# Weights of a block's mixing part split ahead of time, inside the FFN before it, and kept in DRAM

## The chip, the cores and the metric

The kernel runs on one core of a Trainium2 chip. The metric is the time of one execution on the device in microseconds (us), less is better. The core's engines run side by side, each through its own list of instructions in order: TensorE (PE) multiplies matrices, VectorE (DVE), ScalarE (ACT) and GpSimd (POOL) work elementwise, and SyncE (SP) does nothing but issue DMA transfers. POOL's queue issues a few DMAs as well.

## The reference, cut to what matters

Two transformer blocks run one after the other on 512 latent tokens of 1024 features, in float32, each of two layers. Block 1 is window and full attention with modulation and a SwiGLU FFN; it also carries 256 context tokens through its first layer. Block 2 is, for each layer:

```
hn = rms_norm_2(h, attn_norm[l]);  proj = hn @ w_in[l]
y_a = rwkv7_mixer(proj[..., :RW_IN], ...)                  # 4 heads, a recurrence over tokens
y_b = retention_mixer(proj[..., RW_IN:RW_IN+RET_IN], ...)  # 4 heads, chunks of 128
y_c = mla_mixer(proj[..., RW_IN+RET_IN:], ..., w_q_up[l], w_kv_up[l])   # 8 heads, causal
h = h + concatenate([y_a, y_b, y_c]) @ w_out[l]
hn = rms_norm_2(h, ffn_norm[l]);  gu = hn @ w_gate_up[l]
h = h + (silu(gu[..., :D_FF_2]) * gu[..., D_FF_2:]) @ w_down[l]
```

The first half of this, up to the product with `w_out`, is called the mixing stage below; `D_FF_2` is 2816, which is 22 tiles of 128.

## The kernel before

Every projection is done as three products of rounded operands: a weight w is split into a high part (rounded to the matmul's format) and a low part (the rest), the activations likewise, and TensorE sums hi·xh, hi·xl and lo·xh. A weight tile is 128 x kt x 128; with kt = 8, which most have, it is 512 KB and takes 24 matmuls of 128x512. `load_w` (line 129) fetches one: SP's DMA brings it into one of RAW_BUFS = 2 staging buffers `raw`, ACT casts it into `whi` (line 140), DVE subtracts `raw - whi` into `wlo` (line 141). There are W_BUFS = 3 slots for `whi` and `wlo` each, and an instruction that writes into a slot waits until the slot's last readers are done; the raw buffer is free again when line 141 has read it.

The **FFN** (`ffn`, line 919) takes the 22 tiles of its inner dimension in two parts, PARTS2 = 14 and 8. For each inner tile it loads a gate and an up tile (two `load_w`), multiplies both (48 matmuls of 128x512 in the FFNs spoken of here), and `swiglu` turns the two results into a split activation on ACT, DVE and, in block 2, POOL. Behind each part, `residual` multiplies the part's activations by the down weights, 8 output tiles.

The **mixing stage** of block 2 fetches its weights through a list: `orders(l)` names 33 tiles in the order of their use, `order_w` sets the list, and `next_w` (line 148) returns the next tile and keeps three fetched:

```
while self.coming and len(self.loaded) < 3:
    self.loaded.append(self.load_w(self.coming.pop(0)))
return self.loaded.pop(0)
```

Seven more (`w2in` tiles 6, 2, 3, 0, 1, 4, 5, the inputs of the RWKV part) go through `w2proj` straight to `load_w`. Of the 40 tiles of a layer 30 are 512 KB, four (`w2kn`) 128 KB, six (`w2qr`, `w2qn`) 192 KB. The last eight, `w2out`, are the product with `w_out`; three of these are held half multiplied in the banks `b` before the last inputs are there, and finished together (line 1950).

Within an engine the order of the instructions is the order in which the program issues them; waits between engines and for DMAs come from the tiles' readers and writers. The layers' FFNs are spread over the time as follows: the FFN of block 1's layer 1 takes 1508 to 1926 us, block 2's first mixing stage from there to about 2230, its FFN 2258 to 2630, the second mixing stage to about 2930, and the last FFN the rest.

Of the kernel before, what the change touches and what calls it, by code (L numbers as in the profile page):

```python
# [10 lines left out]
F32 = mybir.dt.float32  # L11
F32R = mybir.dt.float32r
# [10 lines left out]
KD = 8  # L23
# [4 lines left out]
TM_BUFS, QS_BUFS, RAW_BUFS, W_BUFS = 5, 3, 2, 3  # L28
# [11 lines left out]
class Seg:  # L40


    def __init__(self, key, off, n):
        self.key, self.off, self.n = key, off, n
        self.v = 0 if key == "lat" else 1
# [12 lines left out]
class Kern:  # L58
    def __init__(self, tc, d, out, ctx, V):
        self.tc, self.nc, self.d, self.out = tc, tc.nc, d, out  # L60
        self.ctx, self.V = ctx, V
        nc = self.nc
        self.uid = 0
        E = ctx.enter_context
        self.const = E(tc.tile_pool(name="const", bufs=1))
        self.wp = E(tc.tile_pool(name="wp", bufs=2))
        self.tmp = E(tc.tile_pool(name="tmp", bufs=2))
        self.dram = E(tc.tile_pool(name="dram", bufs=1, space=DRAM))
        c = self.const
        self.vec = c.tile([128, d["vec"].shape[1]], F32, name="vec")  # L70
        nc.sync.dma_start(out=self.vec, in_=d["vec"])
        self.cf = c.tile([128, d["cf"].shape[1]], F32, name="cf")
        nc.sync.dma_start(out=self.cf, in_=d["cf"])
        self.ident = self.cf[:, 0:128]
        self.ones = self.cf[:, 128:129]
        self.bones = self.cf[:, 129:131]
        self.nhalf = self.cf[:, 131:139]
        self.identb = c.tile([128, 128], BF16, name="identb")
        nc.vector.tensor_copy(self.identb, self.ident)
        self.mge = c.tile([128, 128], BF16, name="mge")  # L80
        self.mle = c.tile([128, 128], BF16, name="mle")
        for o, m in ((0, self.mge), (128, self.mle)):
            t = self.tm(128)
            nc.sync.dma_start(out=t, in_=d["cm"][:, o:o + 128])
            nc.vector.tensor_copy(m, t)
        self.ahead = []
        self.banks = {}
        self.lo = "vector"
        self.lb = itertools.cycle("lb")
        self.pend = []  # L90
        self.stream = "L"


    def pool(self, es, name, side=None):
# [46 lines left out]
        getattr(self.nc, self.lo).tensor_tensor(lo, raw, hi.bitcast(F32), op=ALU.subtract)  # L141
        return hi, lo

    def order_w(self, aps):

        self.coming, self.loaded = list(aps), []

    def next_w(self):

        while self.coming and len(self.loaded) < 3:  # L150
            self.loaded.append(self.load_w(self.coming.pop(0)))
        return self.loaded.pop(0)

    def split(self, x, hi, lo):
# [755 lines left out]
    def ffn(self, wgu, wd, H, x, gcol, segs, start, last, parts, done, ada=0, scales=None, norm=None, after=None, pre=None, angles=False):  # L910


        bc = None
        f0 = 0
        keys = [s.key for s in segs]
        for pi, nf in enumerate(parts):
            with ExitStack() as es:
                pool = self.pool(es, "act")
                act = self.feat(pool, nf, keys, F32R, "ah"), self.feat(pool, nf, keys, F32R, "al")
                wait = []  # L920
                todo = [(f, segs) for f in range(nf)]
                if pi == 0:
                    todo = start + todo[1 + max((f for f, _ in start), default=-1):]
                for i, (f, sg) in enumerate(todo):
                    wg, wu = (self.ahead.pop(0) if self.ahead else self.load_w(wgu[f0 + f, i]) for i in range(2))
                    for s in sg:
                        pg, pu = self.bank()[:, :s.n], self.bank()[:, :s.n]
                        self.proj([(wg[0], wg[1], range(KD))], H, s, pg)
                        if norm:
                            next(norm)  # L930
                        self.proj([(wu[0], wu[1], range(KD))], H, s, pu)
                        if norm:
                            next(norm)
                            norm = None
                        wait.append((s, f, pg, pu))
                        if scales:
                            bc = next(scales)
                            if bc is None:
                                continue
                            scales = None  # L940
                        for s, f_, pg, pu in wait:
                            self.swiglu(s, pg, pu, bc, s.of(act[0], f_), s.of(act[1], f_))
                        wait = []
                    if f0 + f > 1:
                        self.ada_some(ada)
                    if angles and f0 + f == 2:
                        self.angles()
                end = pi == len(parts) - 1
                if callable(gcol):
                    gcol = gcol()  # L950
                self.residual(lambda n, k0, kn: wd[n][:, f0 + k0:f0 + k0 + kn], nf, act, x, gcol,
                              last if end else self.plan(segs), done if end else None, after() if end and after else None, pre if end else None)
                f0 += nf
# [16 lines left out]
    def block1(self):  # L970
        nc, d = self.nc, self.d
        es_ada = ExitStack()
        self.adap = self.pool(es_ada, "ada", "right")
        for l in range(2):
            segs = [LAT, CTX] if l == 0 else [LAT]
            keys = [s.key for s in segs]
# [105 lines left out]
            if l == 0:  # L1082
                def after():
                    nonlocal A, sh
                    A, sh = self.mod_cols(1, 0)
                    return self.mod_norm(X, accs, LAT, A, sh, H, "b", "b")

                self.ffn(d["wgu0"], d["wd0"], H, X, gt, segs, start, self.plan(segs, segs, 5), [7, 7, 8], done, ada=3, norm=norm, after=after,
                         pre=lambda: self.ahead.append(self.load_w(d["wqk1"][0])))
            else:  # L1090
                gf, ga = (self.vec[:, self.V[nm]:self.V[nm] + KD] for nm in ("final", "attn_norm"))
                g = self.one(self.const, [128, KD], F32, "gfa")
                nc.vector.tensor_tensor(g, gf, ga, op=ALU.mult)
                self.acc = self.one(self.tabp, [128, T], F32, "acc2")
                self.acc2 = [accs["lat"], self.acc]
                done = lambda s, n: self.prepare(s, n, X, g, H, [(accs["lat"], None), (self.acc, gf)], True)
                self.xd = self.dram.tile([KD, 128, T], F32, name="xd")
                self.ffn(d["wgu1"], d["wd1"], H, X, gt, segs, start, self.plan([LAT]), PARTS2, done, norm=norm, angles=True)
            es_ps.close()
        self.X = X  # L1100
# [141 lines left out]
        return self.run(self.w2proj_steps(l, j, H, tag, False))  # L1242

    def w2proj_steps(self, l, j, H, tag=None, ordered=True):
        w = self.next_w() if ordered else self.load_w(self.d[f"w2in{l}"][j])
        ps = self.bank(tag or next(self.lb))
        yield from self.proj_steps([(w[0], w[1], range(KD))], H, LAT, ps)
        return ps
# [451 lines left out]

    def orders(self, l):

        d = self.d
        w = d[f"w2in{l}"]
        return ([w[16], w[17], w[18], w[13]] + [d[f"w2kn{l}"][p] for p in range(4)] + [w[14], d[f"w2kvv{l}"], w[15], w[7]]
                + [d[f"w2qr{l}"][p] for p in range(2)] + [d[f"w2qn{l}"][p] for p in range(4)] + [w[9], w[8], w[10]]
                + [d[f"w2v{l}"][c] for c in range(2)] + [w[11], w[12]] + [d[f"w2out{l}"][n] for n in range(KD)])

    def retention(self, l, pool, src, mix):

# [130 lines left out]
    def block2(self):  # L1841
        nc, d = self.nc, self.d
# [27 lines left out]
        for l in range(2):  # L1870
# [89 lines left out]
            def token_scales():  # L1960
                r = self.inv_sqrt(self.token_sums([self.acc], "b")[:, 0:4], 1.0 / 1024)
                yield None
                self.spread(r, "b", bcf)
                yield bcf

            nxt = gcols("attn_norm", 1) if l == 0 else None
            if l == 0:
                done = lambda s, n: self.prepare(s, n, X, nxt, H, [acc], True)
                self.ffn(d[f"w2gu{l}"], d[f"w2d{l}"], H, X, None, [LAT], [], self.plan([LAT]), PARTS2, done, scales=token_scales())
            else:  # L1970
# [217 lines left out]
```

## Time and profile before

| | |
|---|---|
| median of 3 runs | 3361.28 us (3359.95 to 3367.67) |
| profiled execution | 3356.82 us |
| its span, first to last instruction | 3355.1 us |
| PE busy | 3281.2 us (98%) |
| DVE busy | 1901.4 us (57%) |
| ACT busy | 1231.0 us (37%) |
| POOL busy | 355.9 us (11%) |
| DMA, mean | 115 GB/s |

Busy is the time in which an engine worked on an instruction; the share is of the span. The profiled execution lies 1.5 us above its span and 4.5 us under the median of the runs. The DMA share of a stretch, used further down, is the mean busy share of the core's 16 DMA engines in it.

### The profile page before, as it was taken

The numbers are of one execution on the slowest core, as the hardware profiler recorded it, in microseconds if no ns is written. First come the engines' busy times: TensorE is split into PE (matmuls) and PEld (weight loads), VectorE is DVE, ScalarE is ACT, GpSimd is POOL, SyncE is SP. The second block draws the span as 40 slices with busy tenths as digits, with TensorE's granted clock in tenths as the row PEclk, the third lists the DMA queues.
The fourth block names the chain that finished last, engine by engine and source line by source line (L and its number), as shares of the span: only waits on it lengthen the run. The fifth ranks groups of instructions, "written<-read, shape, count | busy, mean of one in ns | idle before, by whom it ended". The sixth has DMA issues, their size and how long they took to land. (4 is left out here: it accounts for less than half of the span.)

```text
span 3355.1 us, 48931 instructions
## 1 busy us (share of the span) xinstructions
PE 3281.2 (98%) x19460; PEld 2741.7 (82%) x19460; DVE 1901.4 (57%) x3324; ACT 1231.0 (37%) x2192; POOL 355.9 (11%) x340
## 2 busy tenths in 40 slices
PE   7999999999999999999999999999999999999998
PEld 4888888888888888889888877778888777788887
DVE  4767765756444567757333466764434566754343
ACT  3566632311212346734222432542223332632222
POOL 0131100100000101101000211121001101121001
PEclk9999999999999999999999999999999999999999
DMA  5533372334434243253232323433333323422322
GB/s 205 147 125 119 114 266 106 114 119 132 126 126 132 76 135 110 93 181 115 94 91 98 123 71 105 130 100 93 91 94 100 109 68 98 133 94 94 91 98 82
DMA packets 137533, 385.86 MB, mean 115 GB/s; under 512 B 17428, under 2 KB 29204, under 8 KB 137304
## 3 DMA queue, kind: packets, MB, share of 16 engines
q1 hardware_dynamic: 133976, 372.15, 35.0%
q0 software_dynamic: 3328, 10.57, 1.0%
q8 instruction: 153, 2.51, 0.3%
q14 instruction: 76, 0.62, 0.1%
HBM read 331.56 MB, written 43.76 MB: 112 GB/s over the span
## 5 line engine op out<-in xcount | busy, mean ns | idle before, releaser
L140 ACT CAST whi<-raw 128x1024 fp32r<-128x1024 f32 (+4 forms) x432 | 435.0, 1008 | 1265.0 <-PE b L159 825.4
L141 DVE TENSOR_TENSOR wlo<-raw,whi 128x1024 fp32r<-128x1024 f32 (+4 forms) x427 | 508.6, 1192 | 379.6 <-ACT whi L140 372.5
L159 PE MATMUL b<-hh,whi 128*128 128x512 f32 (+1 forms) x1760 | 686.8, 390 | 0.0
L159 PE MATMUL b<-hh,wlo 128*128 128x512 f32 (+1 forms) x1760 | 686.0, 390 | 0.0
L159 PE MATMUL b<-hl,whi 128*128 128x512 f32 (+1 forms) x1760 | 681.7, 387 | 0.2 <-POOL hl L251 0.2
L159 PEld LDWEIGHTS b<-hh,whi 128*128 128x128 f32 x1760 | 332.3, 189 | 74.1 <-issue 4.6
L159 PEld LDWEIGHTS b<-hl,whi 128*128 128x128 f32 x1760 | 332.2, 189 | 73.3 <-issue 0.6
L159 PEld LDWEIGHTS b<-hh,wlo 128*128 128x128 f32 x1760 | 332.1, 189 | 72.3 <-issue 0.3
L159 PE MATMUL b<-ah,whi 128*128 128x512 f32 (+1 forms) x864 | 316.7, 367 | 0.0
L159 PE MATMUL b<-al,whi 128*128 128x512 f32 (+1 forms) x864 | 316.5, 366 | 0.0
L159 PE MATMUL b<-ah,wlo 128*128 128x512 f32 (+1 forms) x864 | 316.3, 366 | 0.0
L967 DVE TENSOR_TENSOR tm<-tm,b 128x512 f32<-128x512 f32 (+1 forms) x112 | 70.0, 625 | 206.1 <-PE b L159 200.1
L159 PEld LDWEIGHTS b<-ah,whi 128*128 128x128 f32 x864 | 163.0, 189 | 28.1
L159 PEld LDWEIGHTS b<-ah,wlo 128*128 128x128 f32 x864 | 163.0, 189 | 28.0
L159 PEld LDWEIGHTS b<-al,whi 128*128 128x128 f32 x864 | 163.0, 189 | 27.9
L428 DVE SCALAR_TENSOR_TENSOR wlo<-raw,silb 128x1024 f32<-128x1024 f32 x128 | 158.7, 1240 | 36.6 <-DMA raw<-in_ada1b 20.1
L159 PE MATMUL l<-hh,whi 128*128 128x512 f32 (+1 forms) x472 | 176.7, 374 | 0.9 <-DVE stB L717 0.3
L159 PE MATMUL l<-hh,wlo 128*128 128x512 f32 (+1 forms) x472 | 173.1, 367 | 0.5 <-DVE wlo L141 0.5
L159 PE MATMUL l<-hl,whi 128*128 128x512 f32 (+1 forms) x472 | 173.1, 367 | 0.0
L528 DVE TENSOR_TENSOR pt<-t,pt 128x384 fp32r<-128x384 f32 (+2 forms) x272 | 131.1, 511 | 35.8 <-ACT pt L527 34.1
L159 PE MATMUL b<-hc,whi 128*128 128x256 f32 x800 | 145.4, 283 | 0.0
L159 PE MATMUL S<-kst,qst 128*128 128x256 f32 (+2 forms) x576 | 138.2, 344 | 2.9 <-DVE S L568 1.2
(558 smaller groups left out, 5673.1 us busy)
## 6 DMA issues: line engine op xcount, KB each, us to landing
raw<-in_wgu SPq DMA_DIRECT2D x92, 512.0 KB, 3.3
raw<-in_w2gu SPq DMA_DIRECT2D x88, 512.0 KB, 3.4
raw<-in_ada1b SPq DMA_DIRECT2D x48, 512.0 KB, 3.3
raw<-in_w2in SPq DMA_DIRECT2D x38, 512.0 KB, 3.7
raw<-in_ada0b SPq DMA_DIRECT2D x32, 512.0 KB, 3.8
raw<-in_wg SPq DMA_DIRECT2D x32, 512.0 KB, 3.8
raw<-in_w2d SPq DMA_DIRECT2D x32, 512.0 KB, 3.5
raw<-in_wd SPq DMA_DIRECT2D x24, 512.0 KB, 3.6
```

The source lines that it names most:

```text
L140: self.nc.scalar.copy(hi, raw)
L141: getattr(self.nc, self.lo).tensor_tensor(lo, raw, hi.bitcast(F32), op=ALU.subtract)
L159: self.nc.tensor.matmul(out, l, r, start=start, stop=stop)
L428: nc.vector.scalar_tensor_tensor(junk, raw, 0.5, self.silb[:, v], op0=ALU.mult, op1=ALU.mult, accum_out=m[:, w, k, v:v + 1])
L528: nc.vector.tensor_tensor(o, src, h.bitcast(F32), op=ALU.subtract)
L967: nc.vector.tensor_tensor(b, th, pu, op=ALU.mult)
```

## The change

In two FFNs, that of block 1's layer 1 and that of block 2's layer 0, each inner tile from the third on (20 of 22) is followed by `halve_some(2)`: two tiles of the next mixing stage are loaded and split by `load_w` as before, into the same raw buffers and slots, and POOL's queue writes the high and the low part to DRAM (`kh`, `kl`). So all 40 tiles of a layer are split in the FFN before it. In the mixing stage `load_k` takes the place of `load_w`: two DMAs of SP bring the high and the low part from DRAM straight into a slot of `whi` and one of `wlo`, with no raw buffer, no cast and no subtraction. The other FFNs, which have nothing to split, and block 1 are as before.

```
+        self.halves, self.to_halve = {}, []
...
+    def halve_some(self, n):
+
+        for _ in range(min(n, len(self.to_halve))):
+            key = self.to_halve.pop(0)
+            w = self.load_w(self.weight(key))
+            kept = self.halves[key] = [self.dram.tile([128, w[0].shape[1], 128], F32, name=f"{nm}_{'_'.join(map(str, key))}") for nm in ("kh", "kl")]
+            for a, b in zip(kept, w):
+                self.nc.gpsimd.dma_start(out=a, in_=b.bitcast(F32))
...
+    def load_k(self, key):
+
+        kept = self.halves[key]
+        kt = kept[0].shape[1]
+        w = [self.t(self.wp, [128, 8, 128], F32R, nm, W_BUFS)[:, :kt] for nm in ("whi", "wlo")]
+        for a, b in zip(w, kept):
+            self.nc.sync.dma_start(out=a.bitcast(F32), in_=b)
+        return w
...
-            self.loaded.append(self.load_w(self.coming.pop(0)))
+            self.loaded.append(self.load_k(self.coming.pop(0)))
...
                     if f0 + f > 1:
                         self.ada_some(ada)
+                        self.halve_some(2)
...
+                self.to_halve = [("w2in", 0, j) for j in (6, 2, 3, 0, 1, 4, 5)] + self.orders(0)
                 self.ffn(d["wgu1"], d["wd1"], H, X, gt, segs, start, self.plan([LAT]), PARTS2, done, norm=norm, angles=True)
...
-        w = self.next_w() if ordered else self.load_w(self.d[f"w2in{l}"][j])
+        w = self.next_w() if ordered else self.load_k(("w2in", l, j))
...
+                self.to_halve = [("w2in", 1, j) for j in (6, 2, 3, 0, 1, 4, 5)] + self.orders(1)
                 done = lambda s, n: self.prepare(s, n, X, nxt, H, [acc], True)
                 self.ffn(d[f"w2gu{l}"], d[f"w2d{l}"], H, X, None, [LAT], [], self.plan([LAT]), PARTS2, done, scales=token_scales())
```

Three places in the lists of instructions show the order that comes out of it. The name of a buffer carries a running number; what an instruction waits for stands behind it (DMAHW a DMA of SP, DMASW one of POOL's queue). The first place is ACT's list in the FFN of block 1's layer 1, from the middle of an inner tile on. Before:

```order
L140 CAST whi_15928<-raw_15926 128x1024 [waits DMAHW7_49,PE_49,Activation_49]
L155 CAST ah_15405<-tm_15792 128x512 [waits DVE_49]
L140 CAST whi_15934<-raw_15932 128x1024 [waits DMAHW0_49,PE_49,Activation_49]
L963 ACTIVATE tm_15919<-b_15869 128x512 [waits PE_49]
L140 CAST whi_15997<-raw_15995 128x1024 [waits DMAHW1_49,PE_49,Activation_49]
```

and now:

```order
L141 CAST whi_15948<-raw_15946 128x1024 [waits DMAHW1_49,PE_49]
L141 CAST whi_15958<-raw_15956 128x1024 [waits DMAHW2_49,PE_49,Activation_49]
L988 ACTIVATE tm_15939<-b_15889 128x512 [waits PE_49]
L141 CAST whi_15968<-raw_15966 128x1024 [waits DMAHW3_49,DMASW4_49,DVE_49]
L141 CAST whi_15974<-raw_15972 128x1024 [waits DMAHW4_49,DMASW6_49,DVE_49]
L179 CAST ah_15406<-tm_15940 128x512 [waits DVE_49]
L141 CAST whi_16037<-raw_16035 128x1024 [waits DMAHW5_49,PE_49]
L988 ACTIVATE tm_16028<-b_15978 128x512 [waits PE_49]
L141 CAST whi_16047<-raw_16045 128x1024 [waits DMAHW6_49,Activation_49]
L141 CAST whi_16057<-raw_16055 128x1024 [waits DMAHW7_49,DMASW0_49,DVE_49]
```

Two casts an inner tile have become four: 15948 and 15958 are tiles of the mixing stage, 15968 and 15974 the gate and up tiles of the next inner tile. These two go into the slots that 15948 and 15958 had, and so wait for their writes to DRAM (DMASW4, DMASW6). The writes stand in POOL's list, at the same inner tile:

```order
L152 DMA kh_w2in_3_15952<-whi_15948 128x1024 [waits Activation_49]
L152 DMA kl_w2in_3_15953<-wlo_15949 128x1024 [waits DVE_49]
L152 DMA kh_w2in_0_15962<-whi_15958 128x1024 [waits Activation_49]
L152 DMA kl_w2in_0_15963<-wlo_15959 128x1024 [waits DMASW7_49,DVE_49]
L152 DMA kh_w2in_1_16041<-whi_16037 128x1024 [waits DMASW0_49,Activation_49]
```

They are new, and are issued in the order in which the casts and subtractions are done. The third place is SP's list at the end of block 2's first mixing stage, where the first three `w2out` tiles are in the slots and the fourth comes. Before, its raw load (`raw_21308`) stands 34 rows ahead of these rows, which fetch the fifth to the seventh:

```order
L1926 DMA tm_21261<-mix_17981 128x512 [waits DMAHW0_49,DVE_49]
L134 DMA raw_21389<-in_w2out 128x1024 [waits DMAHW1_49,DVE_49]
L134 DMA raw_21426<-in_w2out 128x1024 [waits DMAHW2_49,DVE_49]
L134 DMA raw_21463<-in_w2out 128x1024 [waits DMAHW1_49,DVE_49]
```

and now the fourth itself stands here, in two DMAs:

```order
L1951 DMA tm_21593<-mix_18381 128x512 [waits DMAHW3_49,DVE_49]
L165 DMA whi_21638<-kh_w2out_3_17856 128x1024 [waits DMAHW4_49,PE_49]
L165 DMA wlo_21639<-kl_w2out_3_17857 128x1024 [waits DMAHW5_49,PE_49]
L165 DMA whi_21664<-kh_w2out_4_17935 128x1024 [waits PE_49]
L165 DMA wlo_21665<-kl_w2out_4_17936 128x1024 [waits DMAHW7_49,PE_49]
L165 DMA whi_21715<-kh_w2out_5_17945 128x1024 [waits DMAHW0_49,PE_49]
```

What waited for a raw buffer (DVE) now waits for a slot, that is for the matmuls of the tile that was in it (PE).

## Rows read from the trace of the kernel before

**Rows 1.** The page: busy time, share of the span, instructions of each engine

```profile
PE 3281.2 (98%) x19460; PEld 2741.7 (82%) x19460; DVE 1901.4 (57%) x3324; ACT 1231.0 (37%) x2192; POOL 355.9 (11%) x340
```

**Rows 2.** Stretches: length, busy time of each engine, clock, DMA share, GB/s

```profile
core 0: us, PE busy (x) PEld busy (x) DVE busy (x) ACT busy (x) POOL busy (x), PEclk, DMA share, GB/s
1580.00:1711.00 131.00, 131.00 (x574) 105.95 (x574) 51.25 (x60) 36.90 (x48) 0.00 (x0) 1.00 0.30 99
...
1940.00:2112.00 172.00, 164.97 (x1695) 126.02 (x1694) 115.84 (x283) 53.37 (x89) 16.98 (x22) 1.00 0.30 90
2112.00:2230.00 118.00, 109.50 (x761) 90.11 (x762) 86.52 (x184) 65.14 (x158) 16.96 (x13) 1.00 0.38 111
2640.00:2930.00 290.00, 274.17 (x2412) 215.14 (x2411) 192.91 (x459) 116.68 (x245) 37.69 (x37) 0.96 0.33 98
14.00:24.00 10.00, 9.06 (x36) 5.42 (x36) 1.64 (x4) 0.72 (x2) 1.02 (x1) 1.00 1.03 411
440.00:492.00 52.00, 49.07 (x281) 42.52 (x280) 39.83 (x68) 16.47 (x31) 0.00 (x0) 1.00 0.90 304
800.00:1000.00 200.00, 200.00 (x1157) 177.24 (x1156) 101.29 (x156) 42.26 (x60) 0.00 (x0) 1.00 0.41 132
```

**Rows 3.** Timeline of ACT, block 1's second FFN: start, duration, instruction [idle before]

```profile
1594.87 0.61 ACT L155 CAST ah<-tm 128x512 fp32r<-128x512 f32 x1
1599.51 1.05 ACT L140 CAST whi<-raw 128x1024 fp32r<-128x1024 f32 x1 [4.03 <-issue]
...
1606.07 0.61 ACT L155 CAST ah<-tm 128x512 fp32r<-128x512 f32 x1
```

**Rows 4.** Timeline of DVE there

```profile
1600.59 1.22 DVE L141 TENSOR_TENSOR wlo<-raw,whi 128x1024 fp32r<-128x1024 f32 x1 [3.77 <-ACT whi L140]
```

**Rows 5.** DMA issues, whole execution: count, KB each, median us to landing

```profile
raw<-in_wgu SPq DMA_DIRECT2D x92, 512.0 KB, 3.3
...
raw<-in_w2out SPq DMA_DIRECT2D x16, 512.0 KB, 4.4
...
y0a<-yt POOLq DMA_DIRECT2D x4, 384.0 KB, 2.6
...
y0b<-yt POOLq DMA_DIRECT2D x4, 384.0 KB, 3.6
```

**Rows 6.** DMA in 430 to 492 us, a busy stretch: total, issues

```profile
DMA packets 7304, 19.00 MB, mean 306 GB/s; under 512 B 768, under 2 KB 1792, under 8 KB 7301
...
raw<-in_ada0b SPq DMA_DIRECT2D x7, 512.0 KB, 4.1
gl<-gates SPq DMA_DIRECT2D x4, 768.0 KB, 6.5
raw<-in_wp SPq DMA_DIRECT2D x6, 512.0 KB, 4.5
```

**Rows 7.** DMA issues in 800 to 1000 us, block 1's first FFN

```profile
raw<-in_ada1b SPq DMA_DIRECT2D x25, 512.0 KB, 3.3
```

**Rows 8.** DVE, first mixing stage, by line: count, busy, mean ns, idle

```profile
L141 DVE TENSOR_TENSOR wlo<-raw,whi 128x1024 fp32r<-128x1024 f32 x21 | 26.4, 1257 | 17.5 <-ACT whi L140 17.5
```

**Rows 9.** Waits of PE in the first mixing stage: total us, times, longest

```profile
PE l L159 <- DVE wlo L141: 0.4, 1, 0.4
```

**Rows 10.** Chain that ended last, in the second mixing stage: start, us, what

```profile
2812.68 1.06 ACT whi L140
2813.76 1.23 DVE wlo L141
...
2842.02 1.23 DVE wlo L141
...
2859.24 0.94 ACT whi L140
```

**Rows 11.** Timeline of PE where the fourth w2out tile begins

```profile
2229.48 0.40 PE L159 MATMUL b<-ml,whi 128*128 128x512 f32 x1
...
2230.63 0.50 PE L159 MATMUL b<-mh,wlo 128*128 128x512 f32 x1
```

More of the change, by code (lines that the diff above doesn't have):

```diff
@@ L142, in load_w, with weight, order_w @@
         return hi, lo
-    def order_w(self, aps):
-        self.coming, self.loaded = list(aps), []
+    def halve_some(self, n):
[5 more added lines that the diff above has]
+                self.nc.gpsimd.dma_start(out=a, in_=b.bitcast(F32))
+    def weight(self, key):
+        name, l, i = key
+        w = self.d[f"{name}{l}"]
+        return w if i is None else w[i]
+    def load_k(self, key):
[5 more added lines that the diff above has]
+        return w
+    def order_w(self, keys):
+        self.coming, self.loaded = list(keys), []
     def next_w(self):
         while self.coming and len(self.loaded) < 3:
-            self.loaded.append(self.load_w(self.coming.pop(0)))
+            self.loaded.append(self.load_k(self.coming.pop(0)))
         return self.loaded.pop(0)
@@ L1701, in orders @@
     def orders(self, l):
[L1703 to L1707, printed above, removed]
+        w = lambda *j: [("w2in", l, i) for i in j]
+        some = lambda nm, n: [(nm, l, i) for i in range(n)]
+        return (w(16, 17, 18, 13) + some("w2kn", 4) + w(14) + [("w2kvv", l, None)] + w(15, 7) + some("w2qr", 2) + some("w2qn", 4)
+                + w(9, 8, 10) + some("w2v", 2) + w(11, 12) + some("w2out", KD))
     def retention(self, l, pool, src, mix):
```

## The prediction

> **What bounds the kernel now.** I read the page first: PE is busy in 98% of the span, DVE in 57%, ACT in 37% [rows 1]. So time can be gained only where PE waits, and lost wherever something new makes it wait. Then the stretches, because the average hides where the 2% lie. In the FFN of block 1's layer 1, 131 us hold 131.00 us of PE: nothing to gain there, and ACT (36.90) and DVE (51.25) have room. The first mixing stage holds 164.97 of 172 and 109.50 of 118 us, so PE is idle for 7.0 + 8.5 = 15.5 us; the second 274.17 of 290, so 15.8 [rows 2]. What the change can gain is at most these two idle times. What it can lose is in the two FFNs, where PE has no gap and 80 tiles' worth of work is put in.
>
> **What it removes: the splits in the mixing stages.** Per stage 40 casts and 40 subtractions go. The 21 large subtractions in the first stage are 26.4 us of DVE [rows 8], a fifth of its busy time there [rows 2]. But work of DVE is not time of PE: of PE's waits in that stage only one is put down to a split, for 0.4 us [rows 9]. The splits act in another way, by standing in the queues of DVE and ACT ahead of small steps of the RWKV recurrence, on which PE waits. The chain of waits shows that: it covers the second half of the second mixing stage (from 2784 us on), and has four pieces of splits in it, 1.06 + 1.23 + 1.23 + 0.94 = 4.5 us [rows 10]. Twice that for the whole stage is 9; when a piece leaves the chain, the next late thing (another step of the recurrence on DVE, or a transfer through DRAM) takes some of its place, and I take two thirds: 6 us a stage. The bounds are 0 (the one wait of 0.4) and 15.5 (all of the idle time).
>
> **What it changes in the mixing stages: the loads.** A tile now comes in two transfers instead of one, 17.4 MB more in about 290 us (30 x 0.524 + 4 x 0.131 + 6 x 0.197), some 60 GB/s on top of 98 where 411 have been moved [rows 2]: hidden, while three tiles are fetched ahead. The cost is that a tile can't be fetched at all until a slot is free; before, the raw buffer took it early. That bites where three slots are let go at once, at the fourth `w2out` tile, whose two DMAs now wait for the last matmuls of the first three. Each of these ends with three matmuls, one tile behind the other, so the first slot is free six matmuls, 6 x 0.233 = 1.4 us, before PE wants the fourth. The high part lands 3.3 us after that, with little beside it [rows 5], the low part behind it: 2 x 0.524 MB at 411 GB/s are 2.55 us, and 3.3 less the 1.28 that 0.524 MB take is 2.0, so 4.6. PE uses the low part only in its third matmul, 0.47 us on: 4.6 - 1.4 - 0.5 = 2.7 us of idle. Before, the same place has 1.15 us from the one start to the other for three matmuls that take 0.70 [rows 11], a loss of 0.45. So about +2.3 a stage; bounds 0, if PE has another wait there anyway, and 4.4 (both parts landing in the 4.4 of `w2out` now [rows 5], one after the other). A stage then gives -6 + 2.3 = -3.7, both **-7.4 us**.
>
> **What it adds in the FFNs.** Per inner tile two more tiles go through the two raw buffers, so each buffer carries two loads a tile. A buffer is in use from the issue of its load until the subtraction has read it, and only then is the next load issued. With R the time to landing, the cast 1.05 us [rows 3], the subtraction 1.23 [rows 4, 10] and 0.04 between them, one use is R + 2.32, and an inner tile can't take less than 2 x (R + 2.32). PE needs 11.2 us for its 48 matmuls (the same ACT instruction at 1594.87 and at 1606.07 [rows 3]). So R decides:
> - R = 3.3, as gate and up tiles land now [rows 5]: 11.24 us, as good as hidden. The lower bound, +0.
> - R = 4.1 to 4.5, as 512 KB land in the stretch that moves 306 GB/s [rows 6]: with 4.3, 13.24 us, +2.0 a tile.
>
> Which R applies follows from the load: an inner tile moves eight times 0.524 MB (gate, up, two raw tiles, four writes), 4.19 MB. In 11.2 us that is 374 GB/s, four times the 99 of now [rows 2], and more than any stretch but the first few microseconds has (411 in 14 to 24 us). In 13.24 us it is 317 GB/s, near the 306 in which R was 4.3. The two agree with each other, so I take **+2.0**. For the upper bound: 4.19 MB at 306 GB/s are 13.7 us, and one cast of 1.05 that no longer lies beside a transfer makes it 14.7, +3.5.
>
> The writes themselves are behind this: the slot of a written tile is wanted by the subtraction of the next gate or up tile, R + 1.05 = 5.3 us after the written tile's own subtraction. POOL's queue lands 384 KB in 2.6 and 3.6 us [rows 5]; for 512 KB I take 4.1, the upper of them and half a microsecond, which is 1.2 inside. ACT stays below its limit: four casts and two other instructions an inner tile (4 x 1.05 + 1.2 = 5.4 of 13 us); DVE likewise. But ACT is in order: a cast that waits for its load holds up the activation of the gate result behind it, and through it the release of PE's banks, so the lateness of a load reaches PE by that way also.
>
> The 20 inner tiles with splits are 13 with two large tiles, 4 with a large and a small one, 3 with two small ones: by the order of the list (seven `w2in`, four more, four `w2kn`, and so on). With 2.0, 1.0 and 0 for these an FFN loses 13 x 2.0 + 4 x 1.0 = 30 us, both **+60**; bounds 0, and 2 x (13 x 3.5 + 4 x 1.75) = 105. The `residual` parts have no splits.
>
> **The sum.** 60 - 7.4 = 52.6 us. On the profiled execution, 3356.8, that is 3409.4; it lies 4.5 us under the median of the runs, so on the median 3361.3 + 52.6 = **3414 us**. All bounds to one side give 3361.3 - 31.3 = 3330 and 3361.3 + 105 + 8.8 = 3475.
>
> **The rivals.**
> - *The loads stay hidden, and little changes.* In block 1's first FFN up to three more loads of 512 KB an inner tile run beside the gate and up tiles, and land in 3.3 us all the same [rows 7], with PE at 200 of 200 us [rows 2]. Against it: that stretch moves 132 GB/s, a third of what the split FFNs would. With R of 3.3 to 3.5 an FFN loses 0 to 6 us, and the time is 3361.3 - 7.4 + 0 to 12, 3354 to 3366: no measurable change. [...]
> - *Faster.* The same R, and the mixing stages give more than I take, since a fifth of DVE's work is gone from the stages in which the recurrence runs through DVE. The point from which it decides: 10 us a stage of the 15.5 idle ones, with 2.3 lost at `w2out`; two stages give -15, 3346 us. For it speaks that RWKV steps stand right behind a split in the chain; against it the one wait of 0.4 us [rows 9], and above all that the FFNs must lose nothing.
> - *Much slower: the writes come one at a time.* If POOL's queue starts a write only when the one before has landed, an inner tile needs 4 x 4.1 = 16.4 us, +5.2, and 2 x 4.1 + 2 x 2.5 = 13.2 with one small tile, +2.0. Two FFNs lose 2 x (13 x 5.2 + 4 x 2.0) = 151, and the time is 3361.3 + 151 - 7.4 = 3505 us. For it: the two kinds of POOL writes differ by 1.0 us for the same size [rows 5]. Against it: nothing in the list makes a write wait for its neighbour, only for the one eight before. The Trainium skill (SBUF — State Buffer, section "SBUF: two separate sides") warns that GpSimd can't write the descriptors of its DMAs while DVE runs in a mode that takes both ports, so that such a DMA stands still behind DVE; a subtraction of two tensors is not among the operations that the page names for it, and no run here shows such a stall.
>
> **How the numbers follow.** A change of under 0.3%, 10 us, can't be told from none here (3351 to 3371). My forecast, slower by 10 to about 105 us: 0.68. Much slower, over 105: 0.11. Within 0.3%: 0.11. Faster: 0.10. So faster 0.10, same 0.11, slower 0.79. The range from 3352 to 3470 leaves out most of the faster case and most of the much slower one, together just under 2 in 10; the forecast's own range, from R of 3.7 (2 x 6.02 = 12.04, +0.84 a tile, +25 in all, 3379) to the bandwidth's 13.7 (+2.5 a tile, +75, 3429), is 3379 to 3429.
>
> **What would show it.** In the two FFNs, in the stretches 1580 to 1711 and 2253 to 2375 moved by what is lost before them: an inner tile of 13.2 us instead of 11.2, PE idle before a gate's or up's first matmul, that idle time put down to `wlo` or `whi`, and these to the load of `raw`; gate tiles landing in about 4.3 us; some 317 GB/s; the writes landing within 5.3 us. In inner tiles 8, 12 and 13 no loss. In the mixing stages: no row of line 140 or 141, each about 4 us shorter, and 2 to 3 us of PE idle at the fourth `w2out` tile that waits for a DMA of `kl`. What would make me wrong: landing at 3.3 us in the FFNs (then there is no loss), writes that land late (then the wait at the cast is for POOL's queue, and the tile longer than 14), or a mixing stage that shortens by over 10 us.

## The result and the profile after

The changed kernel takes 3490.1 us (median of 4 runs, 3482.04 to 3490.61) against 3360.6 of the kernel before beside it: a ratio of 1.038, 95% interval 1.0367 to 1.0393, so 129.5 us slower. The forecast was 3414 us (3352 to 3470): the sign was right, the size well outside the range.

The page of the changed kernel, to be held against [rows 1]: the span, the engines, and the software queue, which is POOL's and now carries the writes.

```profile
span 3488.5 us, 49608 instructions
...
PE 3334.2 (96%) x19460; PEld 2767.5 (79%) x19460; DVE 1904.0 (55%) x3324; ACT 1236.8 (35%) x2192; POOL 440.6 (13%) x500
...
q0 software_dynamic: 22912, 80.31, 6.2%
```

PE does the same 19460 matmuls, and is busy 53 us longer: many ran at the lower level of the clock. The rest of the loss is idle time of PE. To see where the time went I compared the start of the same matmul in both traces; in the FFNs PE's list of matmuls is the same. Up to 1570 us of the kernel before the two keep within 2 us. Then the changed kernel falls (times of the kernel before) 61.0 us behind in the first FFN with splits (up to 1930), 7.7 more in the mixing stage (up to 2250), 60.7 in the second FFN (up to 2630), 4.9 in the second mixing stage, and nothing after it. So 121.7 of the 132 us between the traces are in the two FFNs, and the mixing stages give nothing back. I call how much later a matmul starts than in the trace of before its lateness.

Stretches of the changed kernel, columns as in [rows 2]: the two parts of the first FFN, the two of the second.

```profile
1605.00:1745.00 140.00, 121.07 (x468) 93.09 (x469) 60.98 (x70) 46.83 (x60) 21.83 (x41) 0.91 0.70 234
1825.00:1952.00 127.00, 107.25 (x428) 81.94 (x427) 56.18 (x60) 44.43 (x53) 17.02 (x32) 0.95 0.77 263
2310.00:2490.00 180.00, 163.65 (x655) 127.81 (x654) 88.38 (x99) 61.17 (x76) 47.87 (x57) 0.93 0.64 215
2615.00:2721.00 106.00, 88.70 (x330) 66.99 (x329) 55.10 (x57) 38.00 (x44) 23.96 (x33) 0.90 0.79 266
```

Where PE had 131.00 of 131 us, it now has 121 of 140 and 107 of 127, at a granted clock of 0.90 to 0.95 of the full 2.4 GHz. Part of each stretch ran at the lower level, 1.2 GHz, always in or just behind a wait of PE.

What the waits and what the clock cost can be read apart. The same matmuls of the two FFNs, from the third inner tile to the last down product, before:

```profile
1582.70:1926.50 343.80, 343.80 (x1491) 279.33 (x1490) 133.64 (x149) 98.85 (x127) 20.54 (x13) 1.00 0.32 103
2282.00:2629.80 347.80, 347.80 (x1491) 279.76 (x1490) 155.35 (x174) 98.58 (x123) 38.76 (x29) 1.00 0.32 99
```

and in the changed kernel:

```profile
1580.90:1985.70 404.80, 364.18 (x1491) 286.20 (x1490) 171.10 (x188) 133.37 (x164) 62.98 (x97) 0.95 0.66 219
2348.90:2757.50 408.60, 373.90 (x1492) 291.20 (x1491) 195.17 (x212) 131.64 (x161) 85.05 (x109) 0.95 0.66 215
```

Of the 121.8 us between them PE stands idle for 40.6 + 34.7 = 75.3, and for 20.4 + 26.1 = 46.5 it is busy longer with the same matmuls. A granted clock of 0.95 over 813 us is worth about 41 of these 46.5.

### The profile page after: what moved, and what is told of

It reads as the page before. It is cut to its first block, busy times and chain, and to the rows that moved or that the text cites. A ratio compares the mean times of both kernels' runs of the same rounds, so it can differ in the third digit from the quotient of the medians.

```text
span 3488.5 us, 49608 instructions
## 1 busy us (share of the span) xinstructions
PE 3334.2 (96%) x19460; PEld 2767.5 (79%) x19460; DVE 1904.0 (55%) x3324; ACT 1236.8 (35%) x2192; POOL 440.6 (13%) x500
## 5 line engine op out<-in xcount | busy, mean ns | idle before, releaser
L183 PE MATMUL b<-hh,whi 128*128 128x512 f32 (+1 forms) x1760 | 700.6, 398 | 49.4 <-ACT whi L141 49.4
L183 PE MATMUL b<-hh,wlo 128*128 128x512 f32 (+1 forms) x1760 | 698.1, 397 | 18.5 <-DVE wlo L142 18.4
L183 PE MATMUL b<-hl,whi 128*128 128x512 f32 (+1 forms) x1760 | 692.1, 393 | 0.2 <-POOL hl L275 0.2
L511 DVE TENSOR_REDUCE st<-S 128x1 f32<-128x768 f32 (+2 forms) x160 | 121.9, 764 | 33.7 <-PE S L183 32.8
```

What stands on the lines that cost most here:

```text
L183: self.nc.tensor.matmul(out, l, r, start=start, stop=stop)
L511: nc.vector.tensor_reduce(nm, S[:, lo:hi], axis=AX.X, op=ALU.max, negate=True)
```

## Inside one inner tile of the changed kernel

The forecast's loop can be read from three engines' lists, at an inner tile of the first FFN's second part. ACT (start, duration, instruction, idle before and what ended it):

```profile
1863.62 1.04 ACT L141 CAST whi<-raw 128x1024 fp32r<-128x1024 f32 x1 [3.49 <-DMA raw<-in_wgu]
...
1869.62 1.05 ACT L141 CAST whi<-raw 128x1024 fp32r<-128x1024 f32 x1 [1.12 <-DMA raw<-in_w2in]
...
1876.52 1.05 ACT L141 CAST whi<-raw 128x1024 fp32r<-128x1024 f32 x1 [2.41 <-DMA raw<-in_wgu]
```

DVE:

```profile
1864.70 1.23 DVE L142 TENSOR_TENSOR wlo<-raw,whi 128x1024 fp32r<-128x1024 f32 x1 [3.21 <-ACT whi L141]
...
1870.70 1.23 DVE L142 TENSOR_TENSOR wlo<-raw,whi 128x1024 fp32r<-128x1024 f32 x1 [0.87 <-ACT whi L141]
...
1877.82 1.23 DVE L142 TENSOR_TENSOR wlo<-raw,whi 128x1024 fp32r<-128x1024 f32 x1 [2.45 <-DMA kl_w2in<-wlo]
```

SP's issues (the time runs from the first issue of a row to the end of the second):

```profile
1865.95 3.63 SPq L135 DMA_DIRECT2D raw<-in_w2in  x2
1871.95 3.78 SPq L135 DMA_DIRECT2D raw<-in_wgu  x2
1879.07 5.16 SPq L135 DMA_DIRECT2D raw<-in_w2out  x2
```

One raw buffer goes through these rows: DVE has read it at 1864.70 + 1.23 = 1865.93, the next load is issued at 1865.95, cast at 1869.62 and read at 1871.93; the load behind that is issued at 1871.95 and cast at 1876.52. Its subtraction then doesn't start with the cast's end (1877.57) but at 1877.82, when the write of a low part (`kl_w2in`) has landed. Two uses, 1865.95 to 1879.07, take 13.1 us. That is the loop of the forecast at its forecast length, 13.2, and this tile (PE 1864.7 to 1878.0) made PE 2.1 us late, near the 2.0 expected. But it is the shortest of those that lose anything. The eight tiles of this part added 0, 0, 6.3, 2.1, 6.6, 2.6, 3.6 and 5.7 us of lateness. DMA in that part, 1856 to 1950 us (mean busy share in 40 slices, then the median us to landing):

```profile
DMA  9999738999945379985499997389989259998817
...
raw<-in_wgu SPq DMA_DIRECT2D x10, 512.0 KB, 5.2
raw<-in_w2out SPq DMA_DIRECT2D x8, 512.0 KB, 3.8
kh_w2out<-whi POOLq DMA_DIRECT2D x8, 512.0 KB, 5.4
kl_w2out<-wlo POOLq DMA_DIRECT2D x8, 512.0 KB, 6.6
```

The waits from 1850 to 1950 us (total us, times, longest):

```profile
ACT whi L141 <- DMA raw<-in_wgu: 26.6, 9, 6.1
...
PE b L183 <- ACT whi L141: 15.7, 6, 5.6
DVE wlo L142 <- DMA kl_w2out<-wlo: 11.5, 3, 6.2
...
ACT whi L141 <- DMA kh_w2out<-whi: 6.1, 1, 6.1
```

A low part's write lands 6.6 us after its issue, a high part's 5.4, and four of them (two casts and two subtractions lie next to each other) meet the two gate and up loads, which land in 5.2. The three long tiles end in two ways. At the end of the tile that adds 6.6 us a gate's cast waits 6.1 us for a high part's write and the subtraction behind it 6.2 for a low part's; PE waits 5.64 us. The other two end with a late load: the gate's load that closes the tile of 6.3 us is issued at 1856.73, when its raw buffer comes free, and lands 6.8 us later; the first down load behind the tile of 5.7 us takes 7.0. PE behind the first of these waits:

```profile
1895.74 0.80 PE L183 MATMUL b<-hh,whi 128*128 128x512 f32 x1 [5.64 <-ACT whi L141]
...
1898.26 0.63 PE L183 MATMUL b<-hl,whi 128*128 128x512 f32 x1
1898.69 0.63 PE L183 MATMUL b<-hh,wlo 128*128 128x512 f32 x1
...
1899.43 0.39 PE L183 MATMUL b<-hl,whi 128*128 128x512 f32 x1
1899.66 0.39 PE L183 MATMUL b<-hh,wlo 128*128 128x512 f32 x1
```

Behind the wait matmuls start 0.43 us apart, at the lower level of the clock, then 0.23 apart again. The DMA engines, meanwhile, go from 90% and more down to 10 or 20% and back: transfers in a heap, then the splits, with hardly a transfer beside them.

## The theories

1. **Staging** (the forecast's): the two raw buffers, each used twice an inner tile, make the loop.
2. **Slots**: the next gate and up tiles wait until the writes out of their slots have landed.
3. **Bytes**: eight transfers of 512 KB an inner tile are more than the DMA engines move in 11.2 us.
4. For the mixing stages: the splits taken out were worth 6 us a stage (forecast), or had been hidden already.

This table gives the lateness that PE gains within the inner tiles of the two FFNs, in us, worked out as above from each run's trace (without what it gains between the parts, 7.5 us in the changed kernel). The last column stops at the part's last matmul and the second at the first one behind it; up to there the last has 2.9 more in the changed kernel, 1.0 in x_w2, 3.5 in d_act and 1.5 in w_hi:

```
                                         FFN 1         FFN 2
                                     part 1 part 2  part 1 part 2    sum
changed kernel                         32.6   26.9    30.7   24.0   114.2
x_w2     own slots                     26.1   22.5    24.9   21.1    94.6
d_act    writes on ACT's queue         24.7   18.3    30.9   22.9    96.8
x_r2     own raw buffers               12.7   16.8    19.9   16.6    66.0
w_q      a quarter of each write        9.8   15.3    18.5   14.9    58.5
w_hi     high part written only        11.3   10.1    18.1    9.3    48.8
x_r2w2   own raw buffers, 2 slots       2.3   14.9     1.6   15.6    34.4
x_r2w3   own raw buffers, 3 slots       0.5   14.9     0.0   13.1    28.5
f_nowr   no writes                      0.0    0.0     6.0    2.3     8.3
one      one tile per inner tile        0.0    0.0     7.6    0.0     7.6
x_r2w2q  own buffers, quarter writes    1.1    4.0     0.0    0.0     5.1
```

## The experiments

m_only, m_noout, one and x_r2w2 were timed four times or more, the other variants once. The kernel before varied from 3354.8 to 3367.7 us over 21 runs, so a single time is good to some 10 us; the argument goes by the table, which compares traces. In m_only, m_noout, w_q and x_r2w2q the mixing stages read one kept tile in place of all, and in w_hi its low part, as the expectations say, so they measure time alone.

**m_only: the mixing part alone.**

```
-                self.to_halve = [("w2in", 0, j) for j in (6, 2, 3, 0, 1, 4, 5)] + self.orders(0)
+                self.to_halve = [("w2in", 0, j) for j in (6,)]
...
-        kept = self.halves[key]
-        kt = kept[0].shape[1]
+        kt = self.weight(key).shape[1]
+        kept = [k[:, :kt] for k in self.halves["w2in", key[1], 6]]
```

> The mixing part alone: one tile a layer is split and written in the FFN, the other 39 are not; all of the mixing stage's loads read that one tile's two parts (of its size), so the output is not the reference's. Forecast's step (a stage gains 6 and loses 2.3): 3361 - 7.4, 3353 us. Rival (the splits had been hidden, only the wait at the fourth w2out tile stays): 3361 + 2 x 2.8 = 3366. If the longer stages of the changed kernel (+7.7 and +4.9 by the two traces) come from the mixing part itself and not from the clock: 3373.

Measured: 3362.67 us against 3358.86, ratio 1.0013 (1.0002 to 1.0024). The forecast's 7 us of gain are not there. The lateness against the trace of before is flat through both stages up to the fourth `w2out` tile (-2.0 us at 1930, -1.8 at 2210; +2.2 at 2630, +0.8 at 2910), and grows there by 4.0 and 6.5. (Of the 6.5 some 1.5 is no price of the change: m_noout, f_nowr and one, which load these tiles as before, fall behind by 1.5 at the same place.) PE's waits at the first of these two places:

```profile
PE b L183 <- DMA whi<-kh_w2in: 1.8, 1, 1.8
PE b L183 <- DMA wlo<-kl_w2in: 0.8, 1, 0.8
```

**m_noout: the same, with the `w2out` tiles split in the mixing stage as before.**

```
-            self.loaded.append(self.load_k(self.coming.pop(0)))
+            key = self.coming.pop(0)
+            self.loaded.append(self.load_w(self.weight(key)) if key[0] == "w2out" else self.load_k(key))
```

> The mixing part alone as before (one tile a layer is split, all loads of parts read it, so the output is not the reference's), but the eight w2out tiles of each layer are loaded raw and split as in the kernel before. If the wait at the fourth w2out tile is the whole of what the mixing part costs, and the splits of the other 32 tiles had been hidden: same as before within 3 us, 3356 to 3362. If those 32 splits cost what the forecast took (6 us a stage, some 5 without w2out): 3350. This is also what the whole idea could give if the FFNs lost nothing.

Measured: 3360.3 against 3358.85 us, ratio 1.0005 (0.9996 to 1.0014), the same as before. So the wait at the fourth `w2out` tile is what the mixing part costs, and taking away 32 tiles' splits, with the loads that take their place, is worth nothing that can be measured. Its stretches, for the three of the mixing stages in [rows 2]:

```profile
1940.00:2112.00 172.00, 165.14 (x1651) 127.73 (x1649) 95.13 (x254) 34.17 (x63) 16.93 (x22) 0.96 0.45 144
2112.00:2230.00 118.00, 111.37 (x794) 91.13 (x793) 82.78 (x183) 59.97 (x152) 16.39 (x13) 1.00 0.40 126
2640.00:2930.00 290.00, 275.24 (x2418) 216.67 (x2417) 171.74 (x432) 94.94 (x217) 36.05 (x38) 0.96 0.42 138
```

DVE's work fell from 115.84 to 95.13 us in the first of them, but PE's idle time there from 7.0 to 6.9 only; in all three it is 28.3 us where it was 31.4, and the granted clock in the first is 0.96 where it was 1.00; PE is 2.7 us late behind the first stage and 0.1 early ahead of the second one's last `w2out` tiles. So had the FFNs lost nothing, and the wait at `w2out` been avoided in this way, the change would have given nothing that can be measured.

**f_nowr: loads and splits in the FFN, no writes.**

```
...
-            for a, b in zip(kept, w):
-                self.nc.gpsimd.dma_start(out=a, in_=b.bitcast(F32))
...
-            self.loaded.append(self.load_k(self.coming.pop(0)))
+            self.loaded.append(self.load_w(self.weight(self.coming.pop(0))))
```

(and likewise in `w2proj_steps`).

> The loads and splits in the FFNs alone: nothing is written to DRAM, the mixing stages load and split as in the kernel before (so the 80 splits are done twice). Staging (two raw buffers, each two loads an inner tile): with half the traffic R is 3.3 to 3.6, an inner tile 11.2 to 11.8, so 0 to 15 us over before, 3361 to 3376. Slots held by the writes, or bandwidth: both gone with the writes, 3361 to 3366. Over 3390: the two additional casts and subtractions themselves, by their place in the queues, make most of the loss.

Measured: 3378.85 us. The FFNs lose 8 us, in the second one alone; the rest of the 20 us lies outside them (5.9 us of lateness in the first mixing stage, 4.2 in the second). In the stretch of [rows 2]'s first line:

```profile
1580.00:1711.00 131.00, 131.00 (x588) 106.60 (x587) 74.65 (x87) 57.41 (x73) 0.00 (x0) 1.00 0.48 164
```

PE is at 131.00 of 131 with 20 us more of casts and 23 of DVE work beside it, and each raw buffer used twice an inner tile. So the additional loads, casts and subtractions cost next to nothing by themselves. It doesn't tell the theories apart: without the writes the gate tiles land in 3.1 us, and by the forecast's own formula the two raw buffers then take 2 x 5.42 = 10.8 us, less than PE's 11.2. What is needed for the loss is the writes.

**x_r2 and x_w2: own raw buffers, or own slots, for the tiles split ahead.** A pool in the two FFNs, from which `halve_some` takes one of the two (here the raw buffers; in the other run the two slots `whix` and `wlox`):

```
+                if self.to_halve:
+                    self.hp = self.pool(es, "hx")
...
+    def load_h(self, ap):
...
+        raw = self.t(self.hp, [128, 8, 128], F32, "rawx", 2)[:, :kt]
...
-            w = self.load_w(self.weight(key))
+            w = self.load_h(self.weight(key))
```

> As the changed kernel, but the split-ahead tiles have two raw buffers of their own in the two FFNs, so that each of the four carries one load an inner tile. Staging: the FFNs lose 0 to 15 us instead of 121, time 3375 to 3390. Slots (the next gate and up tiles' casts and subtractions wait for the writes out of their slot): the buffers change nothing, 3470 to 3490. Bandwidth (4.19 MB an inner tile): loads start earlier but land later, 3440 to 3480.

> As the changed kernel, but the split-ahead tiles have two whi and two wlo slots of their own in the two FFNs, and the raw buffers are shared as before. Staging: little changes, 3460 to 3490. Slots: the gate and up tiles no longer wait for POOL's writes, most of the 121 us goes, 3380 to 3410. Bandwidth: little changes, 3450 to 3490.

Measured: 3433.19 us with own raw buffers, 3469.3 with own slots. No theory's number came: each takes a part of the 114 us away, 48 and 20. With own raw buffers PE's time goes into the wait for writes in the shared slots (first FFN, second part):

```profile
PE b L194 <- DVE wlo L142: 10.6, 5, 3.8
DVE wlo L142 <- DMA kl_w2out<-wlo: 8.9, 3, 4.9
```

With own slots, which leave the raw buffers' loop as the forecast had it, the gate tiles are late by their loads again, which land beside the writes:

```profile
raw<-in_wgu SPq DMA_DIRECT2D x9, 512.0 KB, 5.1
```

**x_r2w2: both.**

> As the changed kernel, with both: two raw buffers and two slots each of whi and wlo of their own for the split-ahead tiles, in the two FFNs. Waits for buffers (staging and slots) make the loss, and each alone only passes it to the other (two raw buffers alone took 50 of 121 us away, two slots alone 19): gate and up tiles then have the buffers of the kernel before, the FFNs lose 0 to 15 us, time 3360 to 3385. Bandwidth: an inner tile still moves 4.19 MB, at the 320 to 360 GB/s of the busiest stretches 11.7 to 13.1 us, so 15 to 55 us over before, 3380 to 3420.

Measured: 3431.82 against 3362.52 us, ratio 1.0198 (1.0174 to 1.0222). The first parts lose next to nothing now, the second parts still 15 us each. In 1600 to 1650 us:

```profile
1600.00:1650.00 50.00, 50.00 (x216) 40.24 (x215) 28.78 (x36) 22.70 (x31) 12.88 (x24) 1.00 0.88 321
```

PE has no gap there with DMA busy 0.88 of the time, and the gate tiles land in 3.3; the loads of the tiles split ahead may now be issued long before they are used. The time of the run doesn't show it, since the version loses time at three new places. Ahead of 1570 us PE waits 5.8 us, most of it (4.3 us, to 1547.7) for a result that ACT and DVE work on behind the splits of a split-ahead tile, and this tile for its load. At the start of the second FFN's inner tiles 7.8 us are lost, which the table leaves out (7.0 in x_r2w3). And PE waits 12.9 us at the fourth `w2out` tile, because the loads into the own buffers run ahead in SP's list. Before that tile's DMA four of them had to be issued:

```profile
2252.12 14.48 SPq L149 DMA_DIRECT2D rawx<-in_w2in  x4
2266.70 0.38 SPq L176 DMA_DIRECT2D whi<-kh_w2out  x1
```

**w_hi: only the high parts are written.**

```
-            for a, b in zip(kept, w):
+            for a, b in list(zip(kept, w))[:2 if key[::2] == ("w2in", 6) else 1]:
                 self.nc.gpsimd.dma_start(out=a, in_=b.bitcast(F32))
```

> As the changed kernel, but only the high part of each tile is written (of the first tile of a layer both); the mixing stage reads the low part of that one tile for all, so the output is not the reference's. Slots held by the low part's late write (landing 6.2 us, the high part's 3.9): the subtractions no longer wait for a write, the FFNs lose 20 to 45 us instead of 121. Bandwidth: six transfers of eight, 3.15 MB, loss about a third to a half, 40 to 60. POOL's queue with a fixed price for each write: half, 60.

Measured: 3411.75 us, the FFNs at 48.8 of 114.2. That lies in the range given for bytes and just above the one for slots, and decides nothing by itself.

**d_act: the writes on ACT's queue.**

```
-                self.nc.gpsimd.dma_start(out=a, in_=b.bitcast(F32))
+                self.nc.scalar.dma_start(out=a, in_=b.bitcast(F32))
```

> As the changed kernel, but the writes are issued on ACT's queue (a hardware queue) and not on POOL's. If it is the software queue that makes the writes land late (6.2 us for the low part): they land in 3.5 to 4.5, the FFNs lose 60 to 80 us, time 3430 to 3450. If it is the bytes and the buffers: the same landing, 3480 to 3500; ACT also waits with each low part's DMA for the subtraction, behind which its next cast stands, 1.3 us for each of 80 tiles, which may make it up to 60 us slower.

Measured: 3470.64 us, 96.8 in the FFNs: high parts land in 2.9 us in 1600 to 1720 us where POOL's landed in 4.0 (1610 to 1745); the trace has no landings of the low parts. ACT's list now waits with each low part's DMA for the subtraction. The loss falls by 17 us only; what ACT's wait costs, and so how much a hardware queue would give without it, stays open.

**w_q: as many writes, a quarter of the bytes.**

```
+            k = w[0].shape[1] // (1 if key[::2] == ("w2in", 6) else 4) or 1
             for a, b in zip(kept, w):
-                self.nc.gpsimd.dma_start(out=a, in_=b.bitcast(F32))
+                self.nc.gpsimd.dma_start(out=a[:, :k], in_=b[:, :k].bitcast(F32))
```

> As the changed kernel with as many writes at the same places, but each writes a quarter of its tile (the first tile of a layer whole, from which the mixing stage then reads for all tiles, so the output is not the reference's). If the bytes make the loss (landing grows with the load): 0.5 MB of writes in place of 2.1 an inner tile, the FFNs lose 10 to 40 us of the 121, time 3375 to 3405. If the number of the writes does (a fixed price on POOL's queue, a wait for each): 90 to 120 us, 3455 to 3485.

Measured: 3441.04 us, 58.5 in the FFNs, between the two ranges: half of the loss is there without three quarters of the written bytes. Short writes don't land at once (second part of the first FFN):

```profile
kh_w2out<-whi POOLq DMA_DIRECT2D x8, 128.0 KB, 2.3
kl_w2out<-wlo POOLq DMA_DIRECT2D x8, 128.0 KB, 4.1
```

**one: one tile per inner tile.**

```
-                        self.halve_some(2)
+                        self.halve_some(1)
...
+                self.to_halve = self.to_halve[:20]
```

(the tiles that are not in `self.halves` go through `load_w` in the mixing stage).

> One tile is split after each inner tile instead of two, 20 a layer, and the other 20 in the mixing stage as before. An inner tile moves five transfers, 2.6 MB, in place of eight. If the loss goes with the number of tiles: half of 121, 60 us, and 3361 + 60 + 4 = 3425. If it sets in where the transfers of an inner tile no longer fit into its 11.2 us (2.6 MB in 11.2 us are 234 GB/s; three loads through two raw buffers, 3 x (3.6 + 2.3) / 2 = 8.9 us): 5 to 25 us, 3370 to 3390.

Measured: 3365.82 against 3358.85 us, ratio 1.0014 (1.0004 to 1.0025). Half the tiles cost 7.6 us in the FFNs, not half of 114, and less than either expectation. In the first FFN:

```profile
1580.00:1711.00 131.00, 131.00 (x563) 105.40 (x562) 65.20 (x72) 49.01 (x60) 12.85 (x24) 1.00 0.69 227
```

The loss sets in where an inner tile's transfers and waits no longer fit; it isn't a price for each tile.

**x_r2w3 and x_r2w2q: what the second parts still lose.** As x_r2w2 with three slots; as x_r2w2 with w_q's short writes.

> As the version with two raw buffers and two slots of their own for the split-ahead tiles, but three slots. There, the FFNs' first parts lost almost nothing (2.3 and 1.6 us) and the second parts 14.9 and 15.6, in the third to the sixth inner tile. If that is waiting for slots (a cast or a subtraction of a split-ahead tile stands in ACT's or DVE's list, waits for its slot's write, and holds up the gate tile's behind it): the second parts lose 0 to 6 each. If it is the bytes (seven inner tiles with eight transfers of 512 KB in a row): 12 to 16 each as before.

> The version with two raw buffers and two slots of their own, but each write has a quarter of its tile (the first tile of a layer whole, from which the mixing stage then reads for all, so the output is not the reference's). If the second parts' 15 us are the bytes: 0 to 3 each, as 2.6 MB an inner tile fit. If they are waits for slots, which with short writes end after 2 to 4 us: also little, 0 to 5. If the writes' number on POOL's queue keeps it: 8 to 15 each. With the version with three slots, this tells bytes from slots: slots if both are low, bytes if only this one is.

Measured: 3426.26 and 3387.45 us. A third slot leaves the second parts at 14.9 and 13.1; short writes take them to 4.0 and 0. The stretches in which that loss lies, with three slots:

```profile
1835.00:1885.00 50.00, 42.44 (x152) 31.80 (x152) 26.54 (x28) 21.48 (x25) 9.65 (x19) 0.86 0.98 383
2585.00:2635.00 50.00, 42.34 (x168) 31.50 (x167) 29.16 (x33) 21.70 (x25) 13.69 (x20) 0.97 0.93 351
```

and with short writes:

```profile
1835.00:1885.00 50.00, 48.10 (x199) 37.98 (x198) 26.44 (x30) 20.41 (x25) 8.63 (x16) 0.97 0.67 208
2585.00:2635.00 50.00, 50.00 (x215) 40.21 (x214) 27.06 (x30) 17.19 (x23) 8.01 (x6) 1.00 0.41 131
```

With whole writes the DMA engines are busy 0.98 and 0.93 of 50 us, and a third slot changes nothing: bytes. With buffers enough, that is what is left of theory 3, some 28 to 34 us for both FFNs.

## Why the prediction was wrong

- **Its failed step: the FFN's term, +60, counts PE's idle time alone; what the clock costs behind the waits is put at nothing.** Between the two traces the FFNs lose 121.8 us. PE's idle time is 75.3 of them, not far from 60; for the other 46.5 PE is busy longer with the same matmuls, at a granted clock of 0.95 where it was 1.00. This is three quarters of the 62 us by which the term was too small. It goes with the waits: for the same matmuls x_w2 has 64.4 us idle and 38.0 longer busy, x_r2 48.5 and 22.6, x_r2w2 19.5 and 12.5.
- **A second one: "The writes themselves are behind this"**, with 4.1 us taken for the landing of a write and 5.3 allowed. The low parts' writes land in 6.2 (first FFN's first part, 1610 to 1745) and 6.6 us (second part). So the slots, counted as free, became a second wait in the same loop. Own slots alone take 20 us of lateness away, and PE's idle time falls from 75.3 to 64.4: with the slots out of the way the raw loop makes PE wait about as long as forecast. Own raw buffers take 48 away, both 80: the shared buffers of both kinds are 80 to 86 of the 114 us, the bytes most of the rest. The forecast had named writes that land late, with tiles over 14 us, as a sign of being wrong; the 40 tiles with splits take 11.2 + 121.8 / 40 = 14.2 on average.
- **The raw loop's term**, 2.0 us a tile, was right for a tile in which little else waits (13.1 us measured for 13.24), and wrong as the mean: the long tiles lose 5.7 to 6.6, others nothing. By the forecast's working an FFN should lose 30 us; it lost 61. That the idle time's sum comes near 60 is in part luck, since the tiles don't lose evenly as forecast.
- **R = 4.3** from the busiest long stretch [rows 6] was near for all loads (gate tiles 4.7 to 5.2, split-ahead tiles 3.3 to 3.8), but the evenly spread load that it stood for is not there: transfers come in heaps, at 234 and 263 GB/s on average where 317 was forecast, and single loads take 6.8 and 7.0 us. The 374 GB/s that I took to be out of reach isn't: 383 over 50 us in x_r2w3.
- **Tiles with small weights** were to lose nothing. A 128 KB write lands in 4.0 and 4.5 us, nearly as a large one, so the wait for a slot stays; in the first part of the first FFN the tiles around them lost up to 4.6.
- **Mixing, -6 a stage**: wrong. With +2.3 for `w2out` both stages were to give 7.4 us; they lost 7.7 + 4.9. m_noout shows no gain from 32 tiles; so the pieces of splits in the chain of waits [rows 10] probably stood in place of something that would have been late anyway. The 0.4 us of PE's waits [rows 9] was the better row.
- **The fourth `w2out` tile, +2.3**: right in place and mechanism, too small in size. Forecast was an idle time of 2.7; the changed kernel shows 2.5 at the first of the two places (total us, times, longest), most of it for the high part and not for the low one. With some matmuls behind it at the lower clock the place costs 3.8 us, again more than the idle time:

```profile
PE b L183 <- DMA whi<-kh_w2out: 2.0, 1, 2.0
PE b L183 <- DMA wlo<-kl_w2out: 0.5, 1, 0.5
```

- **The rivals.** "Loads stay hidden" and "faster" fell by the FFNs alone. "The writes come one at a time" came nearest in time (3505), but not as I had it: w_q's quarter writes, high part 2.3 us and low part 4.1 after their issue, show that the second of a pair takes longer though it has no more bytes. But it isn't waiting for the first: in nine pairs of w_q the low part was issued only when the high part had landed (2.6 to 3.5 us behind its issue), and still took 3.3 to 4.3 us; and in the eight pairs issued 0.6 us apart or less the two landing times differ by under 0.8 us, as in the pair of 1866 us (the first two lines below; the other two are of 1838 us, issued 2.8 us apart):

```profile
kh_w2out<-whi POOLq DMA_DIRECT2D x1, 128.0 KB, 2.1
kl_w2out<-wlo POOLq DMA_DIRECT2D x1, 128.0 KB, 2.2
...
kh_w2v<-whi POOLq DMA_DIRECT2D x1, 128.0 KB, 2.1
kl_w2v<-wlo POOLq DMA_DIRECT2D x1, 128.0 KB, 3.9
```

  And in w_hi and x_r2 the loss falls by half or nearly so with POOL's queue as it is.

Not settled: why a low part's write mostly takes longer when it is issued 1.3 us or more behind the high part's, and the 6 to 8 us of single waits in the second FFN in f_nowr and one.

## What to carry to other kernels

Before moving work under a full engine, count every use of each buffer that it shares with what feeds that engine, the wait for its write-back too, and put the sum against the time of one step: a loop that fits costs little (one tile an inner tile, +7.6 us), and one that doesn't costs far more than twice that (two tiles, +114). Take a wait of TensorE for more than its length where the granted clock falls behind it: in the changed kernel, x_w2, x_r2 and x_r2w2 each us of waiting in the FFNs brought another 0.5 to 0.6 us of slower matmuls. And see first that what is taken away elsewhere had cost something: a variant that leaves the new costs out, as m_noout, shows what can be won, here nothing. A piece in a chain of waits is not yet a gain; the idle time put down to it is the better bound.

## What the runs showed of the hardware

Of two writes of equal size issued by POOL's queue the second took about 2 us longer to land in the medians (3.9 and 6.2 for 512 KB on the page, 2.3 and 4.1 for 128 KB in w_q); in w_q it took longer even when the first had landed before it was issued, and not when the two were issued 0.5 to 0.6 us apart. Loads and writes together moved 383 GB/s over 50 us in x_r2w3, with the DMA engines 98% busy; 512 KB landed then in 5.9 to 8.2 us. In the FFNs PE's waits of some us, again and again, went with a granted clock of 0.95, and 75.3 us of idle time with 46.5 us more for the same matmuls.
